# Pairing the score products of two work items in the encoder-block kernel, with four score banks and one attention-value bank

## Chip, cores and metric

The kernel runs on one core of one Trainium2 chip. The metric is the device time of one execution in microseconds. Three timed runs of the kernel before the change took 1973.89 to 1974.49 us, with a median of 1974.28 us.

## What is computed

The reference is one layer of a bidirectional encoder block over 2048 tokens of width 1024. Two attention branches (A: windowed, 8 query heads on 2 key heads, with a sink; B: three groups of 8 heads with dilations 1, 4 and 16) are gated, projected, merged and added to the input. Cut to what matters:

```python
h = rms_norm(x, norm_gain[layer])
proj = h @ w_in[layer]
qa, ka, va, qb, kb, vb, ga, gb, mg = jnp.split(proj, split_idx, axis=-1)
...
# banded_attention(q, k, v, ...): used by A, and by each group of B on strided tokens
scores = jnp.einsum('bnqkgd,bnmkd->bkgnqm', qb, kw).astype(jnp.float32)
logits = jnp.where(valid, scores + bias, NEG_INF)
lse = jax.nn.logsumexp(logits, axis=-1)
...
probs = jnp.exp(logits - lse[..., None])
out = jnp.einsum('bkgnqm,bnmkd->bnqkgd', probs.astype(v.dtype), vw)
...
merged = gates[:, :, 0] * br_a + gates[:, :, 1] * br_b
x = x + merged @ w_out[layer]
```

Everything is float32. The kernel splits each operand into a high and a low float16 part and adds three products, so every product of the reference is three on TensorE.

## The kernel before, in words

**Stages.** At the start the input is normalised, transposed on TensorE (L468, into the score banks `s`) and split. Then comes the main part, and last the merge gates, branch projections and output projection, whose products go to the tiles `fps` (L308, L1446, L1651).

**The main part** runs over 14 units: A twice (heads 0 to 3, heads 4 to 7), and B for each of four head pairs with the groups 1, 2, 0 in turn (the group index `g` has dilation 1, 4 or 16 for 0, 1, 2). A unit has 16 blocks of 128 tokens, taken two at a time as a pair: 112 pairs. A pair's projection is 48 matmuls with 384 columns (L650, into `pj`, 24 for each block). What follows a projection (evacuate, square, normalise, split, transpose by DMA into `kq`) runs on the other engines. Between the projections stand "fills", gate projections of 24 matmuls with 512 columns each (L308).

**Work items.** An item is the attention of one block for two heads. B has 16 items per unit, A has 32, so there are 12 x 16 + 2 x 32 = 256. An item runs through these steps:
- `room` (a tile `pr`, L801);
- `logits` (L808): for every piece of keys six matmuls, three for each of its two heads. Each contracts over 64 rows, head 0 in rows 0 to 63 and head 1 in rows 64 to 127 of TensorE. The results stand in two PSUM banks `s`, one for each head;
- `maxima` (L857, VectorE: bias, and the row minimum of the negated scores), `exps` (L865, ScalarE), `hi` and `lo` (L870, L874), `turn` (L880, a transposing DMA into `pt`);
- `values` (L891, TensorE, into a bank `pv`) and `out` (L910, L915 or L919, ScalarE, out of `pv`). After that group 0 of B merges the three groups (`b_merge_q`) and A its sink (`a_merge`), and a `YPart` turns the result on TensorE (L953), gates it, and stores it. The last `YPart` of a chunk sums a maximum on TensorE (`max2`, L194).

**What sets the order.** The order of every engine's queue is written by hand through a heap of planned times. The unit of these times is one pair (48 matmuls of L650, and the fills of that pair). `at(t, f)` puts a step at time t, and `until(t)` emits all steps due before the next matmul of the stream is emitted. So a step's place on TensorE is a place between two projection matmuls. Items are planned at `nxt`, at the earliest 2.887 units (`LS`) after their pair begins, 0.5 units apart in B and 0.25 in A. `LAGS` and `LV` give each step's distance from there: in B 0.042 for `maxima`, 1.829 for `values`; in A 0.019 and 1.111. Every queue is in order, and the SP queue issues all DMAs.

**PSUM.** There are eight banks: `pj` two, `s` three, `pt` one, `pv` two.

**After the main part** TensorE goes on with the first merge-gate products (`fps`). VectorE first works through some 40 small operations on scales (L201 to L1256), which start from the last `max2`. Behind them it makes the sums of weights (L1413) whose end frees the tile for the next weight load (L175).

Of the kernel before, what the change touches and what calls it, by code (L numbers as in the profile page):

```python
# [21 lines left out]
F32 = mybir.dt.float32  # L22
# [5 lines left out]
PSUM = bass.MemoryType.PSUM  # L28
# [38 lines left out]
LAGS = {'A': (-0.21, 0.002, 0.019, 0.144, 0.276, 0.337, 0.417), 'B': (-0.156, -0.001, 0.042, 0.169, 0.19, 0.379, 0.525)}  # L67
# [35 lines left out]
FILLS = ((2, None, (2, 2, 4, 5)), (3, 0, (8, 9, 10, 12)), (4, 1, (17, 18, 20, 21)), (5, 2, (24, 25, 26, 28)), (6, 3, (32, 35, 37, 38)), (7, 4, (40, 41, 42, 44)), (9, 6, (57, 59, 60, 61)), (10, 7, (64, 65, 66, 68)), (11, 10, (88, 89, 90, 92)), (8, 13, (116, 116, 118, 118)))  # L103
XT_BUFS = 14
KQ_BUFS = 3
VT_BUFS = 10
PT_BUFS = 4
N_BIAS_A = 384
N_BIAS_B = 256
# [2 lines left out]
def block_kernel(tc, x, w_units, w_gate, w_mrg, w_brn, w_out, w_bra, gain, qkg, sink, bias_a, bias_b, b_merge, out):  # L112
    nc = tc.nc
    V = nc.vector
    A = nc.scalar
# [9 lines left out]
    main = ExitStack()  # L125
# [160 lines left out]

    gp = main.enter_context(tc.tile_pool(name="gp", bufs=1))
    pj_p = main.enter_context(tc.tile_pool(name="pj", bufs=2, space=PSUM))
    s_p = main.enter_context(tc.tile_pool(name="sp", bufs=3, space=PSUM))
    pt_p = main.enter_context(tc.tile_pool(name="pt", bufs=1, space=PSUM))  # L290
    norm_bank = [lambda: pt_p.tile([128, 512], F32, name="pt")]
    pv_p = main.enter_context(tc.tile_pool(name="pv", bufs=2, space=PSUM))
    order = ExitStack()
    order.enter_context(tc.manual_schedule())

# [94 lines left out]
    def at(t, f, *args):  # L390
        seq[0] += 1
        heapq.heappush(heap, (t, seq[0], f, args))
# [3 lines left out]
    def until(t):  # L396
        while heap and heap[0][0] <= t:
            now[0], _, f, args = heapq.heappop(heap)
            f(*args)
# [112 lines left out]
    def scale_time(t):  # L512
        return X_CH[0] + X_CH[1] * t
# [6 lines left out]
    for t in range(NT):  # L520
        b = X_SQ[0] + X_SQ[1] * t if t < 4 else X_SQ[2] + X_SQ[3] * (t - 4)
# [16 lines left out]
    for c in range(3):  # L538
        b = X_G[c]
# [5 lines left out]
    steps = [(X_W[2] + X_W[4], w_sum, 0), (X_W[2] + X_W[5], w_pow, 0)]  # L545
# [80 lines left out]
    def drain(t):  # L626

        return min(t, NPAIR + 1 + DRAIN * (t - NPAIR - 1))
# [5 lines left out]
    class Pair:  # L634
# [20 lines left out]
        def plan(self, e):  # L655

            for i in range(2):
                at(e[i] - V_ONES, self.v_ones, i)
                for d, f in zip(EVAC, (self.evac_qk, self.v_hi, self.v_lo)):
                    at(e[i] + d, f, i)  # L660
            steps = (self.square, self.stats, self.newton, self.scale, self.gain, self.hi, self.lo, self.swap, self.turn)
            for d, f in zip(NORM, steps):
                at(e[1] + d, f)
# [7 lines left out]
        def v_ones(self, i):  # L671
# [3 lines left out]
            else:  # L675
                vt = wk.tile([128, 2, 130], F16, name="vt", bufs=VT_BUFS)
            G.memset(vt[:, :nv, HD:HD + 1], 2.0 ** -14)  # L677
# [90 lines left out]
    class Item:  # L768
# [18 lines left out]

        def plan(self, s):
            un = self.un
            steps = (self.room, self.logits, self.maxima, self.exps, self.hi, self.lo, self.turn)  # L790
            for d, f in zip(LAGS[un.kind], steps):
                at(drain(s + d), f)
            v = drain(s + LV[un.kind])
            if un.kind == "B" and un.g == 0 and self.i % 2 == 0:
                at(v - .05, self.z_load)
            at(v, self.values)
            at(v + OUT, self.out, v + OUT)
# [7 lines left out]
                z0 = 0 if self.p0 else W  # L805
                G.memset(self.pv[:, :, z0:z0 + w - W], 0.0)

        def logits(self):  # L808
            un = self.un
            q, keys = self.operands()  # L810
            self.sv = [s_p.tile([128, 512], F32, name="s")[:, :self.W] for _ in range(2)]
            nb = 3 if un.kind == "A" else 2
            o = 0
            for kt, k0, w in keys:
                for i, (a, b) in enumerate(((0, 0), (0, 1), (1, 0))):
                    for j in range(2):
                        rows = slice(64 * j, 64 * j + 64)
                        T.matmul(self.sv[j][:, o:o + w], lhsT=q[0][rows, nb * a + (self.h0 + j) // 2, q[1]:q[1] + 128],  # L818
                                 rhs=kt[rows, nb * b + nb - 1, k0:k0 + w], start=(i == 0), stop=(i == 2))
                o += w  # L820
            assert o == self.W
# [100 lines left out]
        def z_store(self):  # L922
            un = self.un
            dst = zd[un.idx][un.g - 1].rearrange("(j d) f -> d j f", d=un.d)[
                self.r, 128 * self.i:128 * self.i + 128, :]
            nc.sync.dma_start(out=dst, in_=self.z[:].rearrange("p h f -> p (h f)"))
            done.add(("z", un.idx, un.g, self.r, self.i))


    class YPart:  # L930
# [168 lines left out]
    for u in range(NU + 1):  # L1099
        t = 8 * u  # L1100
        steps = [(t + W_STEP[0] + B_GAP[0] * i, w_load, u + 1, (i,)) for i in range(4)]
# [28 lines left out]
    for q in range(4):  # L1130
        fill.setdefault(NPAIR + q, []).extend((mg_step, q, k) for k in range(2))

    un, nxt = None, 0.0
    t = 0
    while t < NPAIR or heap or any(k >= t for k in fill):
        u, j = divmod(t, 8)
        steps = [(f, args) for f, *args in fill.pop(t, [])]
        if u < NU:
            if j == 0:
                un = Unit(u)  # L1140
                at(t + .02, un.bias_load)
                at(t + .6, un.scales)
                at(t + .9, un.bias_scale)
            subs = [divmod(2 * j + i, un.n) for i in range(2)]
            pair = Pair(un, subs)
            e = [t + 3.9 / (7.8 + 5.2 * len(steps)), t + 7.8 / (7.8 + 5.2 * len(steps))]
            pair.plan(e)

            new = [(r, b) for r, c in subs for b in ([c - 1] if c else []) + ([c] if c == un.n - 1 else [])]
            items = [Item(un, r, b, h0) for r, b in new for h0 in ((0, 2) if un.kind == "A" else (0,))]  # L1150
            for it in items:
                step = .25 if un.kind == "A" else .5
                nxt = max(nxt, t + LS)
                it.plan(nxt)
                nxt += step
            streams = [(e[0] - t, pair.matmuls, 0, None), (e[1] - e[0], pair.matmuls, 1, None)]
        else:
            streams = []
        streams += [(5.2 / (7.8 * (u < NU) + 5.2 * len(steps)), f, None, args) for f, args in steps]
        pos = t  # L1160
        for share, f, i, args in streams:
            until(pos)
            if args is None:
                mm, after = f(i), ()
            else:
                mm, after = f(*args)
            for k, m in enumerate(mm):
                until(pos + share * k / len(mm))
                m()
            pos += share  # L1170
            for k, a in enumerate(after):
                at(pos + GATE[k], a)
        until(t + .999)
        if t == NPAIR - 2:
            V.tensor_scalar(imh[:], wtiles[NU][2][:], 0.5 / SX, None, OP.mult)
        t += 1
# [424 lines left out]
    steps = [(0, 0), (1, 0), (2, 0), (0, 2), (1, 2), (3, 0), (2, 2), (3, 2)] + [(i, q) for p in (4, 6) for q in (0, 2) for i in (p, p + 1)]  # L1601
# [182 lines left out]
```

## Time and profile before

| what | value |
|---|---|
| median of 3 timed runs | 1974.28 us |
| the profiled execution: first to last instruction (its span; the page gives no other time of it) | 1971.7 us |
| VectorE busy | 1374.9 us (70%) |
| ScalarE busy | 1063.9 us (54%) |
| GpSimd busy | 876.2 us (44%) |
| mean granted TensorE clock | 0.998 |
| main part, from the first score product to the last value product | 112.4 to 1439.1 us |

A row of the timeline gives start, duration, engine, line, operation, written tile <- read tiles, shapes and count. "64*128" ahead of a shape is the part of TensorE's array that a matmul uses. Matmuls overlap, so the distance from one start to the next tells what a matmul costs, and not its duration. A row of the waits has the waiting engine and line, the releaser, the total in us, how many times, and the longest.

### The profile page before, as it was taken

How to read it: one execution, taken by the hardware profiler on the slowest of the kernel's cores; microseconds unless marked ns; L12 is line 12 of the kernel's file. 1: busy time of each engine (PE TensorE's matmuls, PEld its weight loads, DVE VectorE, ACT ScalarE, POOL GpSimd, SP SyncE). 2: the span in 40 equal slices, each digit the busy share in tenths (PEclk: the TensorE clock that was granted, in tenths of full speed). 3: DMA queues.
4: the chain of work that ended last, by engine and by line, in shares of the span. 5: the costliest groups of instructions: out<-in, count | busy, mean ns of one | idle time of the engine just before them, and what ended most of it. 6: DMA issues, size and time to landing. Idle time of an engine off the chain costs nothing.

```text
span 1971.7 us, 41743 instructions
## 1 busy us (share of the span) xinstructions
PE 1952.1 (99%) x14558; PEld 1166.2 (59%) x14558; DVE 1374.9 (70%) x3604; ACT 1063.9 (54%) x2415; POOL 876.2 (44%) x2248
## 2 busy tenths in 40 slices
PE   8999999999999999999999999999999999999999
PEld 5556665567756678556686556875444444444444
DVE  6668776888767776667876887767867657876412
ACT  7457655766555566565666655656534545432100
POOL 4254445454445645446455565545511220232533
PEclk9999999999999999999999999999999999999999
DMA  6249876796747575566666566645821355788863
GB/s 249 80 85 173 176 149 144 140 187 131 171 83 176 111 166 111 105 137 152 136 122 131 124 153 119 130 101 106 165 95 63 111 174 188 219 239 272 261 222 142
DMA packets 542772, 295.75 MB, mean 150 GB/s; under 512 B 411104, under 2 KB 480352, under 8 KB 541280
## 3 DMA queue, kind: packets, MB, share of 16 engines
q1 hardware_dynamic: 542560, 293.08, 61.8%
q8 instruction: 114, 1.87, 0.4%
q14 instruction: 98, 0.80, 0.1%
HBM read 129.91 MB, written 65.27 MB: 99 GB/s over the span
## 4 chain that ended last, share of the span: by engine, by line
PE 90%; DVE 4%; POOL 2%; issue 1%; DMA 1%; ACT 1%; SPq 0%; DVEq 0%; POOLq 0%; ACTq 0%
PE pj L650 41%; PE pj L308 14%; PE fps L308 13%; PE fps L1651 7%; PE s L818 5%; PE fps L1446 5%; PE pv L891 4%; PE pt L953 1%; PE s L468 1%; POOL rs_t L270 1%; DVE rw L716 1%; POOL rs_t L271 0%; DMA xt<-in_x_dram 0%; DVE qss L704 0%; DVE p L874 0%
## 5 line engine op out<-in xcount | busy, mean ns | idle before, releaser
L650 PE MATMUL pj<-wl,XH 128*128 128x384 f16 x1792 | 589.6, 329 | 0.0
L650 PE MATMUL pj<-wh,XH 128*128 128x384 f16 x1792 | 584.6, 326 | 2.7 <-DVE vt L690 2.7
L650 PE MATMUL pj<-wh,XL 128*128 128x384 f16 x1792 | 586.4, 327 | 0.0
L650 PEld LDWEIGHTS <-XH 128*128 128x128 f16 x3584 | 412.0, 117 | 177.3 <-issue 23.6
L857 DVE CUSTOM_DVE_ANT_0 pr<-s,b,ubuf 128x256 f32<-128x256 f32 (+3 forms) x512 | 219.0, 465 | 92.8 <-PE s L818 91.3
L270 POOL TENSOR_TENSOR rs_t<-rs_y 128x8 f32<-128x8 f32 (+2 forms) x345 | 101.7, 295 | 385.5 <-DVE rs_y L261 285.4
L650 PEld LDWEIGHTS <-XL 128*128 128x128 f16 x1792 | 209.5, 117 | 69.4 <-issue 2.1
L874 DVE SCALAR_TENSOR_TENSOR p<-pr,p 128x512 f16<-128x512 f32 (+2 forms) x256 | 183.6, 717 | 24.6 <-ACT p L870 20.8
L669 ACT ACTIVATE rw<-pj 128x256 f32<-128x256 f32 (+1 forms) x224 | 86.8, 387 | 173.2 <-PE pj L650 171.6
L723 POOL TENSOR_TENSOR rw<-rw,g 128x128 f32<-128x128 f32 (+1 forms) x224 | 130.3, 602 | 87.3 <-DVE rw L716 57.0
L870 ACT ACTIVATE p<-pr 128x512 f16<-128x512 f32 (+2 forms) x256 | 159.4, 623 | 7.4 <-DMA pt<-p 0.6
L308 PEld LDWEIGHTS <-wh 128*128 128x128 f16 x960 | 93.7, 98 | 111.7 <-issue 2.0
L308 PE MATMUL fps<-Y,wh 128*128 128x512 f16 x512 | 152.3, 379 | 0.0
L891 PEld LDWEIGHTS <-pt 128*128 128x128 f16 x3024 | 125.5, 97 | 35.0 <-DMA pt<-p 0.5
L308 PE MATMUL pj<-XH,gh 128*128 128x512 f16 x384 | 146.0, 380 | 0.0
L308 PE MATMUL pj<-XH,gl 128*128 128x512 f16 x384 | 145.5, 379 | 0.0
L716 DVE TENSOR_TENSOR rw<-rw,qr 128x512 f32<-128x512 f32 (+1 forms) x112 | 107.7, 961 | 54.3 <-POOL vt L677 37.4
L308 PE MATMUL pj<-XL,gh 128*128 128x512 f16 x384 | 145.5, 379 | 0.0
L1651 PE MATMUL fps<-wt,M 128*128 128x512 f16 (+1 forms) x684 | 145.2, 375 | 0.0
L891 PE MATMUL pv<-vt,pt 128*128 128x65 f16 (+1 forms) x2784 | 131.7, 193 | 0.1
L180 POOL TENSOR_TENSOR wraw<-wraw,gn 128x768 f32<-128x768 f32 (+1 forms) x80 | 111.2, 1396 | 44.7 <-DMA wraw<-in_w_mrg_dram 44.7
L818 PE MATMUL s<-kq 64*128 64x256 f16 (+2 forms) x1992 | 123.1, 242 | 2.7 <-DVE nmB L857 2.0
(243 smaller groups left out, 3473.2 us busy)
## 6 DMA issues: line engine op xcount, KB each, us to landing
wraw<-in_w_units_dram SPq DMA_DIRECT2D x56, 384.0 KB, 4.6
mtd<-mm SPq DMA_DIRECT2D x56, 256.0 KB, 3.9
M<-mtd SPq DMA_DIRECT2D x8, 1792.0 KB, 9.6
mgd<-fg SPq DMA_DIRECT2D x39, 256.0 KB, 2.1
zd<-z SPq DMA_DIRECT2D x128, 66.0 KB, 1.8
zz<-zd SPq DMA_DIRECT2D x64, 132.0 KB, 2.9
xt<-in_x_dram SPq DMA_DIRECT2D x16, 512.0 KB, 8.7
gtd<-yo SPq DMA_DIRECT2D x32, 256.0 KB, 2.7
```

The lines of the kernel that those rows point to most:

```text
L180: G.tensor_tensor(v, v, gn[:, c0:c0 + 2].unsqueeze(2).to_broadcast([128, 2, n]), OP.mult)
L270: G.tensor_tensor(tv, yv, yv, OP.mult)
L308: out.append(lambda w=w, xx=xx, ch=ch, i=i: T.matmul(ps[:], lhsT=w[:, ch, c0:c0 + 128], rhs=xx[:, ch, ts], start=(i == 0), stop=(i == n - 1)))
L650: out.append(lambda lhs=lhs, rhs=rhs, ch=ch, k=k: T.matmul(ps[:, :384], lhsT=lhs[:, ch, :], rhs=rhs[:, ch, :384], start=(k == 0), stop=(k ...
L716: V.tensor_tensor(q, q, self.rr[:, :n].unsqueeze(2).to_broadcast([128, n, HD]), OP.mult)
L723: G.tensor_tensor(q[:, i, :un.nq, :], q[:, i, :un.nq, :], g, OP.mult)
L818: T.matmul(self.sv[j][:, o:o + w], lhsT=q[0][rows, nb * a + (self.h0 + j) // 2, q[1]:q[1] + 128], rhs=kt[rows, nb * b + nb - 1, k0:k0 + w] ...
L857: V.tensor_tensor_reduce(out=self.pv[:, j, self.p0:self.p0 + W], in0=self.sv[j], in1=un.bias[:, self.h0 + j, self.b0:self.b0 + W], scale=I ...
L870: A.activation(self.sp[:, :128 * n], self.pr, AF.Copy, scale=PSC)
L874: V.scalar_tensor_tensor(self.sp[:, 128 * n:], self.pr, PSC, self.sp[:, :128 * n], OP.mult, OP.subtract)
L891: T.matmul(self.po[:, j, :w], lhsT=p[:, n * j + s, :], rhs=un.v[key][:, vh, c0:c0 + w], start=(k == 0 and s == 0), stop=(k == 2 and s == n ...
L1651: mm.append(lambda ch=ch, k=k, w=w, i=i: T.matmul(ps[:, :cols.stop - cols.start], lhsT=m[:, a, ch, k, :], rhs=wt[w][:, b, ch, cols], start ...
```

## The change

The score products of two neighbouring items are emitted together, at the time of the first of the two, and share a pair of banks where both fit into 512 columns. In B (at most 256 columns an item) two items share two banks; in A (384 columns, 256 at the ends) each item gets two banks of its own. The items are gathered over pairs: where a pair yields an odd number of items, as in groups 0 and 1 of B, the last one is held until the next pair. The other steps of an item keep their distances from its own planned time. `s` has four banks and `pv` one; `vt`, the ring of value tiles in SBUF, has 12 in place of 10.

```diff
-VT_BUFS = 10
+VT_BUFS = 12
...
-    s_p = main.enter_context(tc.tile_pool(name="sp", bufs=3, space=PSUM))
+    s_p = main.enter_context(tc.tile_pool(name="sp", bufs=4, space=PSUM))
...
-    pv_p = main.enter_context(tc.tile_pool(name="pv", bufs=2, space=PSUM))
+    pv_p = main.enter_context(tc.tile_pool(name="pv", bufs=1, space=PSUM))
...
-            steps = (self.room, self.logits, self.maxima, self.exps, self.hi, self.lo, self.turn)
-            for d, f in zip(LAGS[un.kind], steps):
+            steps = (self.room, self.maxima, self.exps, self.hi, self.lo, self.turn)
+            for d, f in zip(LAGS[un.kind][:1] + LAGS[un.kind][2:], steps):
...
-        def logits(self):
+        def logits(self, banks, c0):
...
-            self.sv = [s_p.tile([128, 512], F32, name="s")[:, :self.W] for _ in range(2)]
+            self.sv = [b[:, c0:c0 + self.W] for b in banks]
...
+    def logits(items):
+
+        banks, c0 = None, 0
+        for it in items:
+            if banks is None or c0 + it.W > 512:
+                banks, c0 = [s_p.tile([128, 512], F32, name="s") for _ in range(2)], 0
+            it.logits(banks, c0)
+            c0 += it.W
...
-            for it in items:
-                step = .25 if un.kind == "A" else .5
+            step = .25 if un.kind == "A" else .5
+            held_items += items
+            size = 2
+            while len(held_items) >= size:
+                group, held_items = held_items[:size], held_items[size:]
                 nxt = max(nxt, t + LS)
-                it.plan(nxt)
-                nxt += step
+                at(drain(nxt + LAGS[un.kind][1]), logits, group)
+                for it in group:
+                    it.plan(nxt)
+                    nxt += step
```

**First place: TensorE, in the B unit of group 1 for the second head pair.** Before, the first two items of this unit stand apart. A number behind a tile's name tells one buffer from another, so `s_10702` and `s_10703` are the two banks of the first item.

```order
L650 MATMUL pj_10645<-wh_8802,XH_80 128x384
L818 LDWEIGHTS kq_10345
L818 MATMUL s_10702<-kq_10345 128x192
L818 LDWEIGHTS kq_10345
L818 MATMUL s_10703<-kq_10345 128x192
...
L650 MATMUL pj_10645<-wl_8803,XH_80 128x384
...
L818 MATMUL s_10789<-kq_10345 128x256
L818 LDWEIGHTS kq_10345
L818 MATMUL s_10790<-kq_10345 128x256
...
L650 MATMUL pj_10725<-wl_8803,XH_80 128x384
```

After, the same two items follow each other without a projection matmul between, and the second writes the same two banks.

```order
L650 MATMUL pj_10621<-wh_8744,XH_80 128x384
L818 LDWEIGHTS kq_10245
L818 MATMUL s_10685<-kq_10245 128x192
L818 LDWEIGHTS kq_10245
L818 MATMUL s_10686<-kq_10245 128x192
...
L818 MATMUL s_10685<-kq_10245 128x256
L818 LDWEIGHTS kq_10245
L818 MATMUL s_10686<-kq_10245 128x256
L650 LDWEIGHTS XH_80
L650 MATMUL pj_10621<-wl_8745,XH_80 128x384
```

Over the whole program TensorE has 256 such batches of score products before and 128 after, with the same number of matmuls; each batch stands between matmuls over 128 rows.

**Second place: VectorE, the maxima of the same two items, with what each row waits for.** Before, the rows of the second item wait for TensorE (PE) like those of the first.

```order
L857 ISA pr_10688,z_10719<-s_10702,b1_9943,ubuf_70 128x192 [waits PE_49]
L857 ISA pr_10688,z_10719<-s_10703,b1_9943,ubuf_70 128x192 [waits PE_49]
...
L857 ISA pr_10771,z_10811<-s_10789,b1_9943,ubuf_70 128x256 [waits PE_49]
L857 ISA z_10811 128x1
L857 ISA pr_10771,z_10811<-s_10790,b1_9943,ubuf_70 128x256 [waits PE_49]
```

After, the first item's row waits until the last product into its bank is done, which is one of the second item; the second item's rows wait for nothing.

```order
L857 ISA pr_10673,z_10716<-s_10685,b1_9857,ubuf_70 128x192 [waits PE_49]
L857 ISA pr_10673,z_10716<-s_10686,b1_9857,ubuf_70 128x192 [waits PE_49]
...
L857 ISA pr_10778,z_10825<-s_10685,b1_9857,ubuf_70 128x256
L857 ISA z_10825 128x1
L857 ISA pr_10778,z_10825<-s_10686,b1_9857,ubuf_70 128x256
```

**Third place: TensorE at the end of the main part**, from the last value product (`pv`) over the turn of the last `YPart` (`pt<-idf,ya`) and the sum of the last maximum (`pt<-ym,ones`) to the end of the fills. Before:

```order
L891 MATMUL pv<-vw,pt_23372 128x65
L308 LDWEIGHTS wl
...
L308 MATMUL pj<-XH,gl 128x512
L953 MATMUL pt<-idf,ya 128x128 x4
L308 LDWEIGHTS gh
...
L308 MATMUL pj<-XH,gl 128x512
L194 MATMUL pt<-ym,ones 128x1
L308 LDWEIGHTS gh
```

After (the turn's line is L963 there):

```order
L891 MATMUL pv<-vw,pt_23196 128x65
L308 LDWEIGHTS gh
...
L308 MATMUL pj<-XH,gl 128x512
L963 MATMUL pt<-idf,ya 128x128 x4
L308 LDWEIGHTS gh
...
L308 MATMUL pj<-XH,gh 128x512
L194 MATMUL pt<-ym,ones 128x1
L308 LDWEIGHTS gh
```

The three stretches of L308 matmuls into `pj` (between value product and turn, between turn and sum, and from the sum to the end of the fills) are 49, 24 and 24 before, and 30, 43 and 5 after.

More of the change, by code (lines that the diff above doesn't have):

```diff
@@ L1131, in block_kernel @@
         fill.setdefault(NPAIR + q, []).extend((mg_step, q, k) for k in range(2))
-    un, nxt = None, 0.0
+    un, nxt, held_items = None, 0.0, []
     t = 0
```

## The prediction

> **What bounds the kernel now.** I read the page first: busy shares, then the chain that ended last.
>
> ```profile
> span 1971.7 us, 41743 instructions
> PE 1952.1 (99%) x14558; PEld 1166.2 (59%) x14558; DVE 1374.9 (70%) x3604; ACT 1063.9 (54%) x2415; POOL 876.2 (44%) x2248
> PE 90%; DVE 4%; POOL 2%; issue 1%; DMA 1%; ACT 1%; SPq 0%; DVEq 0%; POOLq 0%; ACTq 0%
> L857 DVE CUSTOM_DVE_ANT_0 pr<-s,b,ubuf 128x256 f32<-128x256 f32 (+3 forms) x512 | 219.0, 465 | 92.8 <-PE s L818 91.3
> ```
>
> TensorE is busy from end to end and carries 90% of the chain, so a microsecond taken from its stream is a microsecond of the kernel, as long as the others keep up. L857 reads each score bank once, 512 times, two for an item: 256 items. Next, the waits of TensorE alone.
>
> ```profile
> PE s L468 <- DVE xt L462: 6.5, 3, 3.9
> PE pj L650 <- DVE vt L690: 2.7, 2, 2.4
> PE s L818 <- DVE nmB L857: 2.0, 1, 2.0
> PE s L468 <- DVE XL L475: 1.1, 1, 1.1
> PE fps L308 <- ACT yo L374: 0.9, 1, 0.9
> PE s L818 <- DMA kq<-spl: 0.7, 1, 0.7
> ```
>
> There is little waiting to remove, under 6 us in the main part. What the busy share hides is the price of a batch of score products, so I looked at starts in the timeline. First a batch of one B item, six matmuls with 256 columns on the 64-row half arrays, and one with 128 columns.
>
> ```profile
> 712.43 0.33 PE L650 MATMUL pj<-wh,XL 128*128 128x384 f16 x1
> 712.59 0.33 PE L650 MATMUL pj<-wh,XH 128*128 128x384 f16 x1
> 712.85 0.50 PE L818 MATMUL s<-kq 64*128 64x256 f16 x6
> 713.29 0.35 PE L650 MATMUL pj<-wl,XH 128*128 128x384 f16 x1
> 713.48 0.33 PE L650 MATMUL pj<-wh,XL 128*128 128x384 f16 x1
> ...
> 524.80 0.33 PE L650 MATMUL pj<-wh,XH 128*128 128x384 f16 x1
> 525.06 0.34 PE L818 MATMUL s<-kq 64*128 64x128 f16 x6
> 525.34 0.34 PE L650 MATMUL pj<-wl,XH 128*128 128x384 f16 x1
> ```
>
> Projection matmuls start 0.16 us apart. Ahead of a batch the distance is 0.26, so 0.10 us goes on entry. After it, the next projection comes 0.19 after the first one, 0.03 too late. Inside, the batches take 0.44 and 0.28 us: 128 columns more in six matmuls cost 0.16, so six matmuls with 128 columns are 0.16 of work, and 0.28 - 0.16 = 0.12 is again a price of the batch. Now a batch that already holds twelve, six with 256 and six with 128 columns (an A item at an end of the sequence):
>
> ```profile
> 176.03 0.33 PE L650 MATMUL pj<-wh,XH 128*128 128x384 f16 x1
> 176.28 0.67 PE L818 MATMUL s<-kq 64*128 64x128 f16 x12
> 176.89 0.34 PE L650 MATMUL pj<-wl,XH 128*128 128x384 f16 x1
> 177.06 0.33 PE L650 MATMUL pj<-wh,XL 128*128 128x384 f16 x1
> ```
>
> It takes 0.61 us, where the two batches above take 0.44 + 0.28 = 0.72, and it enters and leaves once (0.25 and 0.17). So what a second run of six pays when it follows the first is its work alone.
>
> **The change, part by part.**
>
> *Batches.* 256 become 128. Each one gone saves 0.10 on entry, 0.11 inside and 0.01 to 0.03 on leaving: 0.22 to 0.24 us. I take 0.225: 128 x 0.225 = **28.8 us** less. The matmuls stay, so nothing else of TensorE's own work moves. Bounds by rounding of the rows: 0.20 to 0.24, 25.6 to 30.7 us. The Trainium skill, "TensorEngine Tiling (Array Packing)", section Tiling Modes, says that changing the tiling mode drains the engine. With the fixed part of a lone matmul from its page "TensorE: Matmul & The Clock Gate", section Single matmul latency (166 ns warm), an estimate is two such drains, 0.33 us a batch and 42 us in all; the rows measure 0.22 to 0.24, and they decide.
>
> *The held item.* In groups 0 and 1 of B an odd item waits for the next pair, so most items of B, and those of the second A unit behind them, are planned 0.5 units later (24 matmuls of 0.16 us, 3.9 us, and what stands between), with their DMAs on SP (`turn`, `z_store`), memsets on POOL and value products. The second item of a group still stands where it could stand before, 2.887 units behind its pair's start, so no score product needs its `kq` earlier; TensorE waited 0.7 us for `kq` in all. On SP and POOL the moved steps pass the projection's own at other places. No row prices that; the nearest are the TensorE waits above, so between -5 and +5 us, and I take 0.
>
> *Four score banks.* A B batch needs the banks of two batches before, over two units of time ago instead of one item ago. The 2.0 us wait for L857 should go: -2. At the start the transposes L468 get a fourth bank too; they waited 1.1 us for one, but 6.5 us for L462, which comes later in the same stretch. I take 0 there, with -1.1 as the end.
>
> *One value bank.* Each value batch now waits until ScalarE has emptied the one before it.
>
> ```profile
> 177.94 0.71 PE L891 MATMUL pv<-vt,pt 128*128 128x65 f16 x18
> ...
> 178.73 0.26 ACT L910 ACTIVATE zz<-pv 128x130 f32<-128x130 f32 x1
> ...
> 181.28 0.71 PE L891 MATMUL pv<-vt,pt 128*128 128x65 f16 x18
> ...
> 359.61 0.23 ACT L684 ACTIVATE vt<-pj 128x64 f16<-128x64 f32 x1 [2.11 <-PE pv L891]
> ...
> 359.88 0.53 PE L891 MATMUL pv<-vt,pt 128*128 128x65 f16 x12
> ```
>
> In A, where they stand closest, ScalarE is done at 178.99 and the next batch starts at 181.28: 2.3 us of margin. In B the batches stand farther apart. At 359.88 a batch starts while ScalarE is still at L684, ahead of the evacuation in its queue, having waited 2.1 us for a value tile to come free. The larger ring `vt` works against that wait, and against this one:
>
> ```profile
> POOL vt L677 <- PE pv L891: 71.3, 19, 8.1
> DVE pr L857 <- PE s L818: 91.3, 120, 2.3
> ```
>
> GpSimd's 71.3 us were not on TensorE's path, so their loss earns nothing by itself. For the single bank I take +1.5 us, between 0 and 5.
>
> *VectorE's wait for scores.* In B the first item's L857 now waits for the second item's products too, 0.16 us (128 columns) to 0.32 us (256) more, in 96 groups: at most 31 us more. The second item's L857 finds its scores ready, which gives back a share of the 91.3 us. VectorE has 30% idle; I take 0, and say under the rivals what it is if that cover is gone.
>
> *Value products in A.* TensorE comes to them about 0.5 us sooner (two batches fewer in 1.1 units). The page has 0.5 us of waiting there in all (L891, released by the transposing DMA), so a few of 64 are tight: +1, between 0 and 3.
>
> *The end of the main part.* The last value batch stands 19 fill matmuls later. Its chain, and the one behind it:
>
> ```profile
> 1438.90 0.36 PE pv L891 x12
> 1439.26 10.58 PE pj L308 x49
> 1449.84 0.44 PE pt L953 x4
> 1450.27 5.18 PE pj L308 x24
> 1455.45 0.13 PE pt L194 x2
> ...
> 1477.99 1.24 ACT wl L219 x4
> 1479.27 0.39 PE fps L194 x2
> ```
>
> ```profile
> 1445.44 0.42 DVE L1054 TENSOR_TENSOR ya<-ya,zz 128x256 f32<-128x256 f32 x1
> ...
> 1461.68 0.38 PE L308 MATMUL fps<-XH,wh 128*128 128x512 f16 x1 [0.92 <-ACT yo L374]
> ```
>
> Value batch to finished operand of the turn: 1445.86 - 1439.26 = 6.6 us. Ten us of fills covered it before, 30 x 5.18 / 24 = 6.5 us will: +0.3 for the wait, between 0 and 2. The sum L194 now comes 43 fills after the turn, which is ample, but only 5 ahead of the end of the fills instead of 24. From it runs a chain without slack: VectorE's scale operations, weight sums, a weight load, squares, then the sum at 1479.27, for which TensorE already waits a little. The chain starts 19 x 5.18 / 24 = 4.1 us later against TensorE's stream, and the products between (`fps`, from 1461.68) do not grow. So **+4.1 us**, between 0 (if the chain has slack that the trace does not tell) and 5.
>
> *Sum:* -28.8 - 2 + 1.5 + 1 + 0.3 + 4.1 = -23.9 us. The profiled span is 1971.7 us, and the median of the timed runs lies 2.6 us above it; I keep that distance: 1974.3 - 23.9 = 1950.4, say **1951 us**, since small waits rather come than go when a stream is tightened by 1.5%.
>
> **The rivals.**
>
> 1. *The single value bank becomes the bound* (slower). Place: the 64 value batches of A, on TensorE. The margin is 2.3 us; each us by which ScalarE's evacuation is later than that stops TensorE. It decides when the evacuations come 2.3 + 23.9 / 64 = 2.7 us later than now. At 3.0 us: 64 x 0.7 = 45 us, 1951 + 45 = 1996 us. For it: ScalarE's queue is in order and waits in places by more than that (2.1 us at 359.61). Against: ScalarE is 54% busy, and such waits came rarely. 4%.
>
> 2. *VectorE's longer wait reaches TensorE.* If L857's extra 0.16 to 0.32 us in 96 groups made VectorE late for L690, which frees the projection banks, TensorE would stop there: about 96 x 0.24 = 23 us, 1974 us. It decides where VectorE has no idle time to lose; TensorE has waited for L690 only twice. The Trainium skill, "PSUM — Partial Sum Buffer", section "PSUM bank collisions raise a hardware error", has the rule behind that longer wait: guard PSUM by the bank, not by the address, so sharing a bank costs the first reader the second writer's time. The trace before, with a bank for each item and head, cannot show it. 5%.
>
> 3. *The change saves only in part.* The twelve matmuls of my row use one pair of banks; A's second item writes two fresh ones. If that pays the price of a batch again, the 32 groups of A save nothing: 32 x 0.225 = 7.2 us, 1958 us. Against: nothing in the rows ties the price to banks, and the two heads alternate between two banks all the time. If every item paid again, only the end's +4.1 and small waits would be left: 1979 us. 10% for the part, 2% for the whole.
>
> 4. *The end costs nothing and the start gains:* 1951 - 4.1 - 1.1 = 1946 us, inside the forecast's own range.
>
> **How the numbers follow.** The forecast with the bounds of its terms (1944 to 1958 us) has 70%; a larger gain, below 1944, 7%; savings in part, or several small waits, 1958 to 1968 us, 12%; VectorE's wait 5%; no saving 2%; the value bank 4%. The range 1943 to 1964 us holds 8 in 10. A measurement of this kernel tells about 0.2%, 4 us, from no change. Faster by more than that is everything below 1970 us: 0.91; within it 0.05; slower 0.04.
>
> **What would show it.** In the profile after, the timeline has 128 batches of score products, a second item's run costs only its work (a group of 192 and 256 columns takes about 0.68 us from its first start to the next projection), and entries stay at 0.10 us over the pitch. TensorE's waits name `pv` for ScalarE only a few times, L857 no more. The sum at the first `fps` L194 waits about 4 to 5 us, behind a VectorE chain that starts some 5 fills ahead of the end. I am wrong if two runs in one batch start as far apart as separate ones, if `pv` or L690 holds TensorE for more than 10 us in total, or if the stretch after the fills grows by more than 6 us.

## The result and the profile after

| kernel | median | runs |
|---|---|---|
| before | 1974.09 us | 4, from 1972.96 to 1974.49 |
| changed | 1961.64 us | 4, from 1959.70 to 1963.03 |

The ratio is 0.9939, with a 95% interval of 0.9925 to 0.9953. The changed kernel is 12.4 us faster, where 23 us were forecast. The profiled execution of the changed kernel is its fastest one, 1959.70 us.

First the page of the changed kernel: its span, the busy shares, and VectorE's group of maxima.

```profile
span 1957.9 us, 41803 instructions
PE 1927.0 (98%) x14558; PEld 1182.1 (60%) x14558; DVE 1373.8 (70%) x3604; ACT 1058.9 (54%) x2415; POOL 873.8 (45%) x2248
...
L857 DVE CUSTOM_DVE_ANT_0 pr<-s,b,ubuf 128x256 f32<-128x256 f32 (+3 forms) x512 | 218.3, 463 | 32.4 <-PE s L818 31.6
```

TensorE's busy time fell by 25.1 us (1952.1 to 1927.0) and the span by only 13.8. So the change took from TensorE nearly what was forecast for the batches, and 11 us came back as idle time of TensorE (1971.7 - 1952.1 = 19.6 before, 30.9 after). VectorE waits for scores 31.6 us instead of 91.3, with the same work to do: the longer wait of the first item's maxima cost it nothing in sum.

The batches, in the timeline. One batch of two B items (192 and 256 columns), and one of A that holds an item of 256 and 128 columns in one pair of banks and the next item in a fresh pair:

```profile
708.49 0.33 PE L650 MATMUL pj<-wh,XH 128*128 128x384 f16 x1
708.75 0.75 PE L818 MATMUL s<-kq 64*128 64x192 f16 x12
709.43 0.35 PE L650 MATMUL pj<-wl,XH 128*128 128x384 f16 x1
...
177.69 1.16 PE L818 MATMUL s<-kq 64*128 64x128 f16 x24
178.78 0.34 PE L650 MATMUL pj<-wl,XH 128*128 128x384 f16 x1
```

From the first score product to the next projection the B batch takes 0.68 us, and its entry takes 0.26, the pitch of 0.16 and 0.10 more. In A one item took 0.61 us before. Two take 1.09, so the second one cost 0.48, the work of its six matmuls with 256 and six with 128 columns (0.32 + 0.16), though it writes fresh banks. (An item of 256 + 128 columns has the 384 of an item inside the sequence. The prediction calls its row of twelve an item at an end; the sums made from it don't change.)

That the price goes with the 64-row matmuls, and not with any change of bank or shape, is told by the value products, which use all 128 rows and also write another bank in another shape. Before:

```profile
359.66 0.38 PE L308 MATMUL pj<-XH,gl 128*128 128x512 f16 x1
359.88 0.53 PE L891 MATMUL pv<-vt,pt 128*128 128x65 f16 x12
360.24 0.38 PE L308 MATMUL pj<-XH,gh 128*128 128x512 f16 x1
```

They start 0.22 us behind the fill, which is the fills' own distance, and the twelve take 0.36 us, 0.03 each. Over the whole trace of before, the median score batch starts 0.10 us later than the distance of the stream would have it, the median value batch 0.00.

Where the rest went shows best in three stretches: to the first projection matmul, from there to the first merge-gate product, and from there to the end. The rows are groups of one line's matmuls, with the first and the last start. Before:

```profile
L650 PE MATMUL pj<-wh,XH x1792: 322/326/382, 80.0 to 1387.5; 128*128 128x384 f16 x200
L308 PE MATMUL fps<-XH,wh x160: 376/379/379, 1461.7 to 1656.5; 128*128 128x512 f16 x160
```

After:

```profile
L650 PE MATMUL pj<-wh,XH x1792: 322/326/363, 81.9 to 1369.5; 128*128 128x384 f16 x200
L308 PE MATMUL fps<-XH,wh x160: 376/379/634, 1442.4 to 1643.0; 128*128 128x512 f16 x160
```

| stretch | before | after | difference |
|---|---|---|---|
| start to first L650 | 80.0 | 81.9 | +1.9 |
| first L650 to first `fps` | 1381.7 | 1360.5 | -21.2 |
| first `fps` to the end | 510.0 | 515.5 | +5.5 |
| span | 1971.7 | 1957.9 | -13.8 |

The waits of TensorE after, whose columns are as before (total, times, longest):

```profile
PE s L468 <- DVE xt L462: 8.5, 4, 3.6
PE fps L194 <- ACT wl L219: 4.5, 1, 4.5
PE pt L194 <- DVE yo L967: 4.1, 3, 2.4
PE pj L650 <- DVE vt L690: 3.3, 4, 1.4
PE pv L891 <- DMA pt<-p: 2.7, 3, 1.5
...
PE pt L194 <- ACT gh L332: 0.7, 2, 0.5
PE pv L891 <- POOL rs_t L272: 0.5, 1, 0.5
PE pv L891 <- ACT zz L915: 0.5, 1, 0.5
PE pj L308 <- DVE vt L690: 0.4, 1, 0.4
PE pv L891 <- ACT z L919: 0.4, 1, 0.4
```

Of the row with `gh`, 0.26 us lie in the main part, and the rest at the start. So the main part has 4.1 + 3.3 + 2.7 + 0.3 + 0.5 + 0.5 + 0.4 + 0.4 = 12.2 us. The same view of before had 2.7 + 2.0 + 0.7 there, and 0.6 for a turn (L953): 6.0. So 6.2 us of waiting came on, and since the stretch lost only 21.2 us, the batches saved about 27.4, by this estimate 0.21 us each. The largest newcomer is a wait that the prediction doesn't name. It is the matmul of a weight norm (L194, into `pt`) behind the output copy of a `YPart` (L967), which reads the same bank:

```profile
515.37 0.69 DVE L716 TENSOR_TENSOR rw<-rw,qr 128x512 f32<-128x512 f32 x1 [2.35 <-POOL vt L677]
515.98 0.74 DVE L967 SCALAR_TENSOR_TENSOR yo<-pt,ubuf,yo 128x512 f32<-128x512 f32 x1
516.78 0.38 PE L194 MATMUL pt<-gsq,ones 128*128 128x1 f32 x2 [2.42 <-DVE yo L967]
```

The planner marks that bank free as soon as it has emitted L967. VectorE comes to it late, since the operation ahead of it in its queue (L716) had waited 2.35 us for GpSimd. TensorE stands at L194 with its whole stream behind.

The end of the main part, in the timeline. The matmuls behind the long wait start 0.43 us apart, where this shape has 0.215 (1458.81 to 1459.03 to 1459.24).

```profile
1459.03 0.38 PE L308 MATMUL fps<-XH,wl 128*128 128x512 f16 x1
1459.24 0.38 PE L308 MATMUL fps<-XH,wh 128*128 128x512 f16 x1
1464.11 0.39 PE L194 MATMUL fps<-wsq,ones 128*128 128x4 f32 x2 [4.48 <-ACT wl L219]
...
1465.12 0.63 PE L308 MATMUL fps<-XH,wh 128*128 128x512 f16 x1
1465.55 0.63 PE L308 MATMUL fps<-XL,wh 128*128 128x512 f16 x1
```

The table by windows has the granted clock as the third number from the end of a row: it is 0.50 here.

```profile
1464.40:1467.80 3.40, 3.40 (x10) 1.22 (x11) 3.19 (x11) 2.37 (x4) 0.00 (x0) 0.50 0.20 77
```

The sum came 21.7 us behind the first `fps` product, against 17.6 before: +4.1 us, and the half clock adds the rest of the +5.5. From the last maximum's sum to this one are 24.0 us in both profiles (1455.29 to 1479.27, and 1440.12 to 1464.11): the chain between them took as long as before and only began later against TensorE's stream.

At the start a wait also grew, with a half clock behind it. Before:

```profile
23.61 0.66 PE L468 MATMUL s<-idf,xt 128*128 128x128 f32 x4 [1.08 <-DVE XL L475]
...
27.50 0.63 PE L468 MATMUL s<-idf,xt 128*128 128x128 f32 x4 [1.93 <-DVE xt L462]
29.19 0.38 PE L308 MATMUL pj<-XH,gh 128*128 128x512 f16 x1
```

After:

```profile
22.80 0.82 PE L468 MATMUL s<-idf,xt 128*128 128x128 f32 x6
23.45 1.47 PE L502 MATMUL pv<-ones 128*128 128x256 f16 x12
28.10 1.11 PE L468 MATMUL s<-idf,xt 128*128 128x128 f32 x4 [3.18 <-DVE xt L462]
31.13 0.38 PE L308 MATMUL pj<-XH,gh 128*128 128x512 f16 x1
```

With a fourth bank the transposes no longer wait 1.08 us. The warm-up products (L502, work without a result that anyone reads) are therefore done earlier, and the wait for the input grows from 1.93 to 3.18 us. Behind it the same work (from the transposes to the fill shown) takes 3.03 us instead of 1.69. So 0.6 us are a later input and 1.3 a half clock (the table by windows has 0.57 from 27 to 31 us, and 1.00 before). The later input belongs to this execution: in the second profile of the changed kernel these transposes start at 26.86, with the same wait of 3.18 us and again a half clock, and the first L650 at 81.0 and not 81.9.

### The profile page after: what moved, and what is told of

Read it like the earlier page. It is cut to its first block, busy times and chain, and to the rows that moved or that the text cites. A ratio compares the mean times of both kernels' runs of the same rounds, so it can differ in the third digit from the quotient of the medians.

```text
span 1957.9 us, 41803 instructions
## 1 busy us (share of the span) xinstructions
PE 1927.0 (98%) x14558; PEld 1182.1 (60%) x14558; DVE 1373.8 (70%) x3604; ACT 1058.9 (54%) x2415; POOL 873.8 (45%) x2248
## 4 chain that ended last, share of the span: by engine, by line
PE 89%; DVE 4%; POOL 2%; DMA 2%; issue 1%; ACT 1%; SPq 0%; DVEq 0%; POOLq 0%; ACTq 0%
PE pj L650 39%; PE pj L308 15%; PE fps L308 13%; PE fps L1666 7%; PE fps L1461 5%; PE s L818 4%; PE pv L891 4%; DMA pt<-p 1%; PE pt L963 1%; PE s L468 1%; POOL rw L723 1%; DVE rw L716 1%; DMA xt<-in_x_dram 0%; POOL rs_t L270 0%; POOL rs_t L271 0%
## 5 line engine op out<-in xcount | busy, mean ns | idle before, releaser
L650 PE MATMUL pj<-wh,XH 128*128 128x384 f16 x1792 | 584.4, 326 | 3.3 <-DVE vt L690 3.3
L650 PE MATMUL pj<-wl,XH 128*128 128x384 f16 x1792 | 586.7, 327 | 0.0
L650 PE MATMUL pj<-wh,XL 128*128 128x384 f16 x1792 | 586.4, 327 | 0.0
L650 PEld LDWEIGHTS <-XH 128*128 128x128 f16 x3584 | 412.8, 117 | 167.5 <-issue 12.1
L650 PEld LDWEIGHTS <-XL 128*128 128x128 f16 x1792 | 208.4, 116 | 73.9 <-issue 1.1
L857 DVE CUSTOM_DVE_ANT_0 pr<-s,b,ubuf 128x256 f32<-128x256 f32 (+3 forms) x512 | 218.3, 463 | 32.4 <-PE s L818 31.6
L723 POOL TENSOR_TENSOR rw<-rw,g 128x128 f32<-128x128 f32 (+1 forms) x224 | 137.6, 633 | 110.2 <-DVE rw L716 80.8
L716 DVE TENSOR_TENSOR rw<-rw,qr 128x512 f32<-128x512 f32 (+1 forms) x112 | 103.7, 926 | 112.0 <-POOL vt L677 86.2
L308 PEld LDWEIGHTS <-wh 128*128 128x128 f16 x960 | 94.2, 98 | 113.4 <-issue 3.5
L308 PE MATMUL fps<-Y,wh 128*128 128x512 f16 x512 | 152.3, 379 | 0.0
L308 PE MATMUL pj<-XH,gh 128*128 128x512 f16 x384 | 146.1, 381 | 0.0
L308 PE MATMUL pj<-XH,gl 128*128 128x512 f16 x384 | 145.8, 380 | 0.0
L308 PE MATMUL pj<-XL,gh 128*128 128x512 f16 x384 | 145.7, 380 | 0.0
L729 ACT ACTIVATE spl<-rw 128x512 f16<-128x512 f32 (+1 forms) x112 | 72.0, 643 | 127.7 <-POOL vt L677 108.7
```

What stands on the lines that cost most here:

```text
L308: out.append(lambda w=w, xx=xx, ch=ch, i=i: T.matmul(ps[:], lhsT=w[:, ch, c0:c0 + 128], rhs=xx[:, ch, ts], start=(i == 0), stop=(i == n - 1)))
L650: out.append(lambda lhs=lhs, rhs=rhs, ch=ch, k=k: T.matmul(ps[:, :384], lhsT=lhs[:, ch, :], rhs=rhs[:, ch, :384], start=(k == 0), stop=(k ...
L716: V.tensor_tensor(q, q, self.rr[:, :n].unsqueeze(2).to_broadcast([128, n, HD]), OP.mult)
L723: G.tensor_tensor(q[:, i, :un.nq, :], q[:, i, :un.nq, :], g, OP.mult)
L857: V.tensor_tensor_reduce(out=self.pv[:, j, self.p0:self.p0 + W], in0=self.sv[j], in1=un.bias[:, self.h0 + j, self.b0:self.b0 + W], scale=I ...
```

## Experiments

Ten kernels ran, each beside runs of the kernel before on the same chip. "Below" is the distance of the two medians.

| kernel | median, runs | before beside it | below | ratio, 95% interval |
|---|---|---|---|---|
| changed, first | 1961.64, 4 | 1974.09 | 12.4 | 0.9939, 0.9925 to 0.9953 |
| changed, again | 1960.32, 5 | 1972.94 | 12.6 | 0.9939, 0.9925 to 0.9952 |
| e1_apart | 1994.44, 4 | 1973.58 | -20.9 | 1.0104, 1.0090 to 1.0117 |
| e2_one_item | 1974.39, 11 | 1973.58 | -0.8 | 1.0001, 0.9993 to 1.0010 |
| e3_tail | 1955.23, 4 | 1973.58 | 18.4 | 0.9903, 0.9889 to 0.9917 |
| e4_warm | 1958.52, 5 | 1973.58 | 15.1 | 0.9920, 0.9906 to 0.9933 |
| e5_gate | 1957.45, 5 | 1972.88 | 15.4 | 0.9928, 0.9914 to 0.9941 |
| e6_lv | 1956.02, 4 | 1972.88 | 16.9 | 0.9912, 0.9898 to 0.9925 |
| e7_all | 1945.44, 4 | 1972.88 | 27.4 | 0.9860, 0.9847 to 0.9874 |
| e8_all_apart | 1974.76, 11 | 1972.94 | -1.8 | 1.0007, 0.9998 to 1.0016 |
| e9_all_one | 1973.34, 11 | 1972.94 | -0.4 | 1.0001, 0.9993 to 1.0010 |

**Holding without sharing a batch.** The first experiment keeps everything of the change but the batch: each item's score products go back to the item's own planned time, and so to two banks of its own.

```diff
-                at(drain(nxt + LAGS[un.kind][1]), logits, group)
                 for it in group:
+                    at(drain(nxt + LAGS[un.kind][1]), logits, [it])
                     it.plan(nxt)
```

> The changed kernel with one thing undone: each item's score products stand at that item's own planned time again, so there are 256 batches and not 128; the held items, the four score banks, the one value bank and the larger value ring stay. Theory (a batch costs TensorE 0.225 us of entry, filling and leaving): 128 x 0.225 = 28.8 us more than the changed kernel, near 1990 us, slower than the kernel before. Rival (most of the gain comes from the banks or the ring): within 8 us of the changed kernel's 1961.6 us. In the timeline the theory wants all batches at 0.10 us entry and bodies of 0.28 to 0.61 us.

It is 33 us above the changed kernel (20.9 + 12.4), where 28.8 were expected. That is the price of 128 batches, and some 4 us on top. The profile names these: its waits in the main part are 14.2 us instead of 12.2, and a half clock from 389.7 to 393.1 us adds up to 1.7. The largest row is that of the value products in A, which wait for their transposed weights 9.5 us in all, not 2.7.

```profile
PE pv L891 <- DMA pt<-p: 9.5, 5, 2.6
...
PE fps L194 <- ACT wl L219: 4.5, 1, 4.5
PE pt L194 <- DVE yo L967: 2.2, 2, 1.3
```

The other two rows say that the late sum at the end, and waits for L967, are there with held items alone, without a shared batch.

**Banks alone.** Here no item is held or paired. Left of the change are the four score banks, the one value bank and the larger ring.

```diff
-            size = 2
+            size = 1
```

> The changed kernel with groups of one item: no item is held, no products are paired; only the banks (four for scores, one for values) and the larger value ring differ from the kernel before. Theory (the small waits that ate part of the gain come from holding items half a unit later, which puts the sums L194 behind the turns of the output parts and the last value batch nearer the end): those waits vanish with the holding, so the time is the kernel before within 3 us, 1972 to 1977 us, with the sum after the fills waiting about 0.5 us. Rival (they come from the single value bank): several us slower than before, 1978 us or more, with value batches waiting for ScalarE over 5 us in all.

The banks alone change nothing in the time that can be measured (ratio 0.9993 to 1.0010). In its profile two small things offset each other. The main part is 0.8 us shorter: the 2.0 us for `nmB` (L857) are gone, but those for L690 are 4.1 instead of 2.7. The start is 1.5 us longer (first L650 at 81.5, not 80.0), with a wait of 3.17 us for the input and a half clock behind it, so that loss belongs to the banks and not to the held items. In the waits the value bank costs one row, 0.5 us, and neither L967 nor the transposing DMA of A appears:

```profile
PE pv L891 <- ACT zz L915: 0.5, 1, 0.5
...
PE fps L194 <- ACT wl L219: 0.4, 1, 0.4
```

So the waits for `yo` and for `pt` come with the held and paired items, and not with the single value bank, which was the rival. At the end the sum waits 0.4 us as before.

**The end.** The sum L194 of the last maximum gets 26 fills behind it instead of 5.

```diff
-... (8, 13, (116, 116, 118, 118)))
+... (8, 13, (116, 116, 118, 119)))
```

> The changed kernel with the last fill matmuls (24 of L308) emitted one unit later, so that 26 of them, not 5, stand behind the last maximum's sum; nothing else differs. Theory (TensorE's 4.6 us wait at the sum L194 after the fills comes from the late start of the scale chain, and the wait halves TensorE's clock for 3.4 us): the wait falls to about 0.5 us, no half clock there, 4.1 + 1.5 = 5.6 us less than the changed kernel, near 1956 us. Rival (the chain behind is late for another reason, such as the weight load): the wait stays and the time is 1961.6 us.

It lies 6.4 us below the changed kernel by the medians (6.0 by the distances to before), and the two intervals don't overlap. The wait at the first `fps` sum is gone from the view. The sum starts at 1459.98 without a wait, and the clock behind it is full (1.00 from 1459.9 to 1464 us).

```profile
1459.98 0.39 PE L194 MATMUL fps<-wsq,ones 128*128 128x4 f32 x2
```

From the last maximum's sum to this one it is 24.0 us again (1436.01 to 1459.98). The gain is 4.1 for the wait and, for the most part, the half clock for the rest.

**The start.** 26 warm-up products instead of 12 fill the time until the input is there.

```diff
-X_WARM = (24, 16, 16, 16, 12)
+X_WARM = (24, 16, 16, 16, 26)
```

> The changed kernel with 14 more filler matmuls in the last group of fillers at the start (26, not 12), which fill a hole of 3.3 us in TensorE's work ahead of the first gate products. Theory (that hole is long enough to halve the granted clock for 3.4 us in some executions, and fourth score bank made it longer): the hole falls to about 1.8 us, the clock stays full there, the time is 0 to 1.5 us less than the changed kernel and its spread smaller. Rival (the hole costs nothing, since VectorE and GpSimd set the start): no difference beyond 0.5 us.

It gained 2.7 to 3.1 us, where 0 to 1.5 were expected. The profile has a wait of 1.65 us where the changed kernel had 3.18, and a full clock behind it (1.00 from 27 to 31 us):

```profile
27.32 0.66 PE L468 MATMUL s<-idf,xt 128*128 128x128 f32 x4 [1.65 <-DVE xt L462]
...
29.05 0.38 PE L308 MATMUL pj<-XH,gh 128*128 128x512 f16 x1
```

From 27.32 to 29.05 are 1.73 us, as before. By the times alone the interval overlaps that of the changed kernel. It is the profile that shows an effect, of 2.1 us (first L650 at 79.8 and not 81.9, of which 0.6 is the later input); that the gain is larger isn't shown.

**The norm sums.** The flag of the projection bank is cleared 0.3 units later.

```diff
-            held[0] = False
+            at(now[0] + .3, held.__setitem__, 0, False)
```

> The changed kernel, but the planner's flag that a projection turn's accumulator is still in use is cleared 0.3 units (about 0.9 us) later than the gate of the turn, so that no norm sum is planned into the bank that turn still occupies. Theory: the waits of TensorE at L194 for VectorE's output copy L967 (0.69, 1.39, 2.58 and 0.42 us in the profile of the changed kernel, 5.1 in all) are waits that the change brought; they go, and the half clock that a wait of about 2.6 us can set off with them: 3 to 6 us less than the changed kernel's 1961.6, so about 1957. Rival: what is late there is the output copy, and any TensorE work behind it waits as long: within 1 us of 1961.6.

3.0 us less than the changed kernel, at the low end of the theory, and the intervals overlap. (Two figures of the expectation are off: the view of the waits has 4.1 us for L967, not 5.1; and since 112 pairs take 1307.5 us from the first L650 to the last, 0.3 units are about 3.5 us, not 0.9.) The waits for L967 have gone from the view. In their place stand 0.9 us for another step of the norm (`wm`, L201) and 3.8 us for the DMA instead of 2.7, so about half of the 4.1 was kept; the main part is 1.9 us shorter (1358.6 against 1360.5).

**The values of A.** They come due 0.149 units later.

```diff
-LV = {'A': 1.111, 'B': 1.829}
+LV = {'A': 1.26, 'B': 1.829}
```

> The changed kernel, but the value products of the first kind of item (A) come due 0.149 units (about 0.45 us) later after their score products. Theory: the four waits of the value products for the transposing DMA (1.16, 0.27, 1.66 and 0.35 us in A, 3.4 in all) go: about 3 us less than the changed kernel's 1961.6, so about 1958.5. Rival: values that come later hold the rings of transposed tiles and the value bank longer, and new waits take the place of the old ones: within 1 us of 1961.6, or above it.

4.5 us less by the distances to before (16.9 against 12.4), more than the 3 expected. (By the same count as above, 0.149 units are about 1.7 us, not 0.45.) The DMA's row fell from 2.7 to 0.3 us, and the sum with L967 from 4.1 to 2.4:

```profile
PE pt L194 <- DVE yo L967: 2.4, 2, 1.9
...
PE pv L891 <- DMA pt<-p: 0.3, 1, 0.3
```

The profiled execution is the slowest of the four, and its main part is only 1.7 us shorter than that of the changed kernel (1358.8), with a half clock behind the wait of 1.9 us. Why the times gained more than the row for the DMA holds is left open.

**All four edits.**

> The changed kernel with four edits together: 26 held-back output projections instead of 5 behind the last norm sum (alone 6.4 us less), 26 warm-up products instead of 12 behind the first loads (alone 3.1 us less), the flag of the projection bank cleared 0.3 units later, and the values of A 0.149 units later. Theory, that the waits found in the profile of the changed kernel are each their own and add up: 1961.6 - 6.4 - 3.1 - 4 - 3, so about 1945. Rival: the planner's order shifts with each of the two last edits and opens other waits as large: 1952, which is the two measured edits alone, or above it.

1945.44 us. The four gains, by distances to before, are 6.0 + 2.7 + 3.0 + 4.5 = 16.2 us, and together they brought 15.0 (27.4 - 12.4). They add up, nearly. The waits for L967, for the DMA of A and at the first `fps` sum are gone from the view; the largest row of the main part is L690 with 1.7 us. Its four runs lie within 1.6 us, those of the changed kernel, in the two sets, within 3.3 and 7.7. This is the best version found, 1.4% below the kernel before.

**What the batch alone is worth.** Two more take the pairing out of that best version: one keeps the items held but each in its own batch (as in the first experiment), the other neither holds nor pairs them (`size = 1`). The changed kernel ran once more beside them.

> The changed kernel as it is, run beside the two next ones for a direct comparison: 1961.6 by its earlier runs, 1959.7 to 1963.0.

> The kernel with the four edits (1945.4), but with the score products of each item at its own planned time, 256 batches again. Theory: with the side waits and the half clocks removed from both, what is left between the two is the price of 128 batches, 28.8 us: 1974, between 1970 and 1977. Rival: one batch for two items also spares waits that these edits don't touch, as between the changed kernel and its version with separate batches, 32.8 us: 1978 or more.

> The kernel with the four edits, but without holding or pairing: every item alone and at the time of the kernel before, four score banks and one value bank. Theory: three of the four edits mend waits that only the held and paired items bring, so they are worth nothing here; the warm-up products take 1.5 to 3 us as they did alone: 1971.5, between 1970 and 1974. Rival: the edits are plain improvements of the kernel, whatever stands beside them, and the 16 us between the changed kernel and the one with the four edits come back here: 1958, and the pairing is worth no more than 13.

The changed kernel came at 1960.32, the same ratio as the first time. With most of the side waits gone, one batch for two items is worth 29.2 us by the medians (27.4 + 1.8), and 27.9 between the fastest runs of the two kernels (1972.81 and 1944.91, both at a mean clock of 0.999). The stretch from the first projection to the first `fps` product says nearly the same. All four edits, paired:

```profile
L650 PE MATMUL pj<-wh,XH x1792: 322/326/360, 79.7 to 1361.2; 128*128 128x384 f16 x200
L308 PE MATMUL fps<-XH,wh x160: 376/379/379, 1434.1 to 1628.4; 128*128 128x512 f16 x160
```

All four edits, apart:

```profile
L650 PE MATMUL pj<-wh,XH x1792: 322/326/527, 79.8 to 1390.2; 128*128 128x384 f16 x200
L308 PE MATMUL fps<-XH,wh x160: 377/379/379, 1463.7 to 1658.1; 128*128 128x512 f16 x160
```

1354.4 against 1383.9: 29.5 us. The waits in it are nearly equal, 6.4 against 6.6 us, but the kernel with separate batches has a stretch at half clock here, which the other lacks and which costs up to 1.7 us (shown in the last section). That leaves about 27.5 us for the batches. The same working gave 27.4 for the changed kernel against the one before, and gives 28.5 against the first experiment (32.3 us between the stretches, less 2.1 of waits and 1.7 of half clock). So a batch costs 0.21 to 0.22 us.

The last kernel shows that the four edits are worth nothing without held and paired items (ratio 0.9993 to 1.0010): they mend what the change broke. It came out within its theory's range but 1.8 us above its figure. Its profile starts the projections 1.3 us earlier than that of the kernel with the banks alone (80.2 against 81.5), and has a wait of 1.7 us just ahead of the first `fps` product that the other lacks (L194 behind L981, at 1453.32).

## Why the prediction was half right

The direction and the mechanism of the gain were right; the size was not. 1961.6 us lies above the forecast with the bounds of its terms (1944 to 1958) and in the branch "savings in part, or several small waits", which had 12%. It was the small waits. That the wider range (1943 to 1964) still holds it is luck: no term of the sum foresaw the largest of them. The bounds of the single terms, all added up, would have reached from 1936 to 1967 us; the narrower range supposes that they offset each other, and here they did not.

- *Batches, -28.8.* Right within its bounds (25.6 to 30.7): 27.4 to 28.5 us, after waits and half clocks are taken out. The 29.2 of the times lies nearer to 28.8 than the rows warrant, since a half clock in the other kernel helped. Entry and body cost what the rows said, and fresh banks in A pay nothing, so the third rival fell. (It counts 32 groups of A with fresh banks; the groups at the two ends of the sequence, two items of 256 columns, share theirs by the kernel's rule, so they are 28.) The first two rivals fell as well: the waits for ScalarE's evacuations out of the single value bank (`zz`, `z`) are 0.9 us, where the forecast had +1.5, and L690 held TensorE for 3.7 us, not for 23.
- *The held item, 0 between -5 and +5.* **This is the step that failed.** The prediction looked for moved work on the queues of SP and GpSimd. It did not ask which bank the moved steps use. A `YPart` holds `pt`, which the norm sums L194 share, and after the change L967 comes late for them: +4.1 us in waits, none in the view of before, and none when no item is held or paired. The term's own bounds hold it, but the value taken was 0.
- *Value products in A, +1 (0 to 3).* Mis-sized: 2.7 us in the waits. Moving them later took nearly all of it away. The reason given, that TensorE comes to them sooner with fewer batches, covers only a part. In the first unit, of A, where no item is held, 0.99 us came on at 130.99 (1.44 in the second profile), and the first experiment has no wait there. The rest lies in the second unit of A behind held items, and there the first experiment, with 256 batches, waits 9.5 us.
- *L857, -2.* The wait for `nmB` is gone, as forecast. But half of it or more came back in the waits for L690: 2.7 us before, 3.7 after, 4.1 with the banks alone.
- *The start, 0 (as low as -1.1).* Wrong in sign. The fourth bank did remove the 1.1 us; the time only moved into the next wait, which grew past 3 us and was followed by a half clock: +1.9, and +1.5 with the banks alone.
- *The end, +4.1 and +0.3.* The mechanism was right to the tenth: the chain has no slack, and the sum came 4.1 us later. What was missing is the half clock behind the wait: +5.5 in all. The +0.3 for the last turn didn't come; no wait of a turn is in the view.

The forecast's sum was -23.9, the two profiled spans show -13.8. Of the 10.1 us between them, 4.1 are L967, 1.9 the start, 1.7 the transposing DMA and 1.1 the end (5.5 against 4.4); the rest is 1.3 us, in which the batches are 1.4 short of 28.8. None of the prediction's own signs of being wrong appeared: a second run in a batch cost its work alone, `pv` and L690 together stayed below 10 us, and the stretch after the fills grew by 5.5, below the 6 that it named. The loss came through waits that no sign covered.

Left open is how much of the loss in the main part belongs to holding and how much to pairing: holding alone has waits for L967 (2.2 us) and for the DMA, but no kernel paired items without holding any; only the 0.99 us in the first unit can be put down to pairing. The edits of the flag and of the warm-up products can't be told from the changed kernel by their own times; their profiles and the sum of the four speak for them.

## What to carry to other kernels

Where TensorE is nearly always busy, count how often it changes between matmuls over 128 rows and over 64, and put those of one kind together: here 0.21 to 0.22 us for each batch saved. Then look, bank by bank, at who else uses what the moved steps hold, because here the loss came mostly from a shared bank and from chains with no slack, not from the engines' load. This change was worth twice as much when distances that were tuned to the old order were set again: 12 us alone, 27 with four small edits.

## What the runs showed of the hardware

Waits of TensorE can cost more than their length. A stretch of 3.4 us at half the granted clock came behind the waits of 3.18 and 4.48 us shown above, and also behind shorter ones. In the first experiment it was a wait of 2.44 us, for the DMA. With the four edits and separate batches it came behind 1.83 us:

```profile
392.61 0.63 PE L891 MATMUL pv<-vt,pt 128*128 128x65 f16 x12 [1.83 <-DMA pt<-p]
```

```profile
392.90:396.30 3.40, 3.40 (x25) 1.88 (x21) 2.63 (x6) 3.40 (x8) 0.00 (x0) 0.50 0.96 218
```

But the wait of 2.42 us at 516.78 in the changed kernel had a full clock behind it. In the second profile of the same kernel the same wait, 2.48 us at 516.51, had a half clock. First the changed kernel, then its second profile:

```profile
517.00:520.40 3.40, 3.40 (x32) 2.53 (x32) 2.82 (x16) 2.25 (x5) 0.16 (x3) 1.00 0.09 19
...
516.30:519.70 3.40, 3.19 (x20) 1.83 (x20) 2.18 (x10) 1.63 (x2) 0.58 (x4) 0.51 0.02 5
```

At this place the experiment with the end had 2.77 us and a full clock, the one with the start 2.50 us and a half clock. So the length alone does not decide between about 1.8 and 2.8 us, and it may go otherwise in the next run: of the five later runs of the changed kernel the slowest had 1965.1 us at a mean clock of 0.994, the fastest 1957.4 us at 0.997. The Trainium skill, "TensorE: Matmul & The Clock Gate", section "Part 1: The HAM clock gate (the "warmup" mystery)", describes a window that runs free, about 3.4 us long, by which the clock is lowered and raised; the length of the stretches here agrees with it. The same page of the Trainium skill, section "HAM oscillation — how this bites in real kernels", gives as a rule that no gap be longer than about 3.4 us. Here gaps of 1.83 and 2.44 us were enough, and the measurement decides. A half clock cost 1.3 us at the start, and by an estimate up to half of 3.4, or 1.7 us, where TensorE is busy throughout.
